# Row statistics of the first token half moved from VectorE to ScalarE in the three generated output projections of a two-layer trunk

## The chip, the cores and the metric

The kernel runs on one NeuronCore of a Trainium2 chip. The metric is the device time of one execution in microseconds (us). The kernel before was timed three times: median 2871.21 us, lowest 2867.52, highest 2874.64. One further execution, the profiled one, took 2872.47 us; every duration below comes from its trace. The engines are called by their short names: PE is TensorE (the matrix engine), DVE is VectorE, ACT is ScalarE, POOL is GpSimd and SP is SyncE, which issues most of the DMAs.

## What is computed

The input `x` has 1024 tokens of width 1024 in float32. It passes two layers. Layer 0 mixes the tokens by a gated delta rule, layer 1 by retention; a convolutional feed-forward block follows in each. Every mixer and every feed-forward block ends in a projection, a scaled residual and a layer norm:

```python
def _standardize(x, eps):
    xf = x.astype(F32)
    mu = jnp.mean(xf, axis=-1, keepdims=True)
    xc = xf - mu
    var = jnp.mean(xc * xc, axis=-1, keepdims=True)
    return xc * lax.rsqrt(var + eps)
...
    for i in range(DEPTH):
        mod = (e @ ada_w[i] + ada_b[i])[:, None, :]
        sh1, sc1, g1, sh2, sc2, g2 = jnp.split(mod, 6, axis=-1)
        y = mixers[i % N_MIXERS](x * (1.0 + sc1) + sh1)
        x = layer_norm(DN_ALPHA * x + (1.0 + g1) * y, ln_g[i, 0], ln_b[i, 0])
        y = conv_ffn(x * (1.0 + sc2) + sh2, ffn_up[i], ffn_conv_w[i], ffn_conv_b[i], ffn_down[i])
        x = layer_norm(DN_ALPHA * x + (1.0 + g2) * y, ln_g[i, 1], ln_b[i, 1])
```

Here `y` is the output of a projection such as `ffn_down` (the last matrix product inside `conv_ffn`) or `ret_w_out` (the last one inside the retention mixer). The change concerns `mu` and `var` of three of the four layer norms: after the feed-forward block of layer 0, after retention, and after the feed-forward block of layer 1, which is the kernel's output.

## The kernel before

**Products.** Every float32 operand is cut into a high part, copied by ACT into a reduced-precision tile (`split`, L89), and a low part, the difference, computed by DVE (L90). Each product of two tiles is then three matmuls (`mma`). A split of a tile of 128 rows and 512 columns is one ACT copy followed by one DVE subtraction, and the matmuls wait for both.

**A projection.** `proj_gen` (L1477 on) computes 1024 tokens by 1024 columns. It uses a form of Strassen's scheme: seven products, called p0 to p6 here, instead of eight. Each product runs over `nj` steps `j` (11 in the feed-forward projections, 8 in the retention projection) of 12 matmuls of 128x512 into four accumulator tiles. `make` prepares the operands of one step: it forms the wanted sum or difference of weight blocks (L1521), splits activations into `ab` and weights into `bb`, and issues the weight load `Br` of three steps further on. The last steps of p6 (`tail`) are held back so that the four row tiles `t` = 0..3 finish one after the other. In the profile the matmuls are L1636.

**The rows' ends.** Tokens come in two halves of 512, each in four row tiles of 128 rows; columns come in two halves `nh` = 0, 1. For each row tile and column half `finish` multiplies by the gate (L1562), adds the scaled residual (L1564) and takes row statistics with BN_STATS (L1565), all on DVE. When both column halves are there, `norm` aggregates them (BN_AGGR, L1570), adds the epsilon (L1571), has POOL raise the result to the power -1/2 (L1572), and normalises the row tile `xt`: on ACT (L321) for the first half of layer 0's projection, on DVE (L323) in the retention projection, and with the output's scale and bias in a mixed way (L1578 to L1586) in the final projection. The first half's column half 0 ends in p2 (p3 in the retention projection), its column half 1 after p4, by a list `later` from which four entries are taken per step of p5. The second half ends with p5 and p6. After that list is empty, `hooks` bring the transposes of the normalised rows (L295), their scaling on ACT (L297) and the splits `hT` for the next stage's matmuls (L110 to L112 in the stage after the retention projection).

**The three calls.** The feed-forward projection of layer 0 lies at about 1160 to 1400 us of the trace, the retention projection at about 2030 to 2230 us, the final one at about 2660 us to the end. They are called the layer-0, the retention and the final projection below. The fourth layer norm uses another function, `proj_ln`, with its own row statistics.

**What sets the order.** The code above is written out by generators; a scheduler of the framework then fixes one static order of instructions for each engine, and each engine runs its own list strictly in that order, waiting by semaphores on the others. So an instruction that is not ready holds up all that stand behind it on its engine. Tiles come from pools of fixed size: `qkv` (20 tiles of 128x512; here `ar`, `Br`, `Bw`, and in the retention projection the sums `c` of L1595), `aux` (`pa`), `cv` (`u2`), and eight banks of PSUM, four of which (`acc`) hold p6 and are then taken over, one by one, by the next stage.

Of the kernel before, what the change touches and what calls it, by code (L numbers as in the profile page):

```python
# [11 lines left out]
AF = mybir.ActivationFunctionType  # L12
ALU = mybir.AluOpType
AX = mybir.AxisListType

P = 128
D = 1024
# [12 lines left out]
LN_EPS = 1e-5  # L30
# [3 lines left out]
def trunk_kernel(ctx: ExitStack, tc, A):  # L34
    nc = tc.nc
    pe, act, dve, pool, sp = nc.tensor, nc.scalar, nc.vector, nc.gpsimd, nc.sync
# [9 lines left out]
    def tl(tag, shape, dt=F32, name=None):  # L46
        return sb.tile(shape, dt, tag=tag, name=name or tag, bufs=BUFS[tag])
# [13 lines left out]
    def mm_tile():  # L61
        return ps.tile([P, HALF], F32, tag="mm", name="mm", bufs=2)

    def sc_tile():
        return ps.tile([P, HALF], F32, tag="sc", name="sc", bufs=2)

    def acc4():
        return [acc_tile(), acc_tile(), acc_tile(), acc_tile()]
# [13 lines left out]
    def hs(half):  # L82
        return slice(half * HALF, (half + 1) * HALF)
# [234 lines left out]
    def normalize(xt, mv, on_act):  # L318
        if on_act:
            dve.scalar_tensor_tensor(mv[:, 2:3], mv[:, 0:1], -1.0, mv[:, 3:4], ALU.mult, ALU.mult)  # L320
            act.activation(xt, xt, AF.Identity, bias=mv[:, 2:3], scale=mv[:, 3:4])  # L321
        else:
            dve.tensor_scalar(xt, xt, mv[:, 0:1], mv[:, 3:4], ALU.subtract, ALU.mult)  # L323
# [483 lines left out]
    def give(tag, n):  # L807
        free[tag] += n
# [468 lines left out]
    c, z = "c", "z"  # L1277
# [199 lines left out]
    def proj_gen(nj, ablk, wsrc, slots, xsrc, G, final, ln_next, tag, ltags, dst, key, mm=pe.matmul, gate=None):  # L1477
# [63 lines left out]
        stats = [[], []]  # L1541
# [15 lines left out]
        def xh(half, t, nh):  # L1557
            x = xts[half][t]
            return x[nh] if isinstance(x, tuple) else x[:, hs(nh)]

        def finish(half, t, nh, c):
            dve.tensor_tensor(c, c, G[nh], ALU.mult)  # L1562
            xv = xh(half, t, nh)
            dve.scalar_tensor_tensor(xv, xv, ALPHA, c, ALU.mult, ALU.add)  # L1564
            dve.bn_stats(stats[half][t][:, nh], xv)  # L1565

        def norm(half, t):
            xt = xts[half][t]
            mv = tl("s8", [P, 4], name="mv")
            dve.bn_aggr(mv[:, 0:2], stats[half][t])  # L1570
            dve.tensor_scalar(mv[:, 2:3], mv[:, 1:2], LN_EPS, None, ALU.add)  # L1571
            pool.tensor_tensor(mv[:, 3:4], mv[:, 2:3], mhalf[:, 0:1], ALU.pow)  # L1572
            if final is None:
                normalize(xt, mv, bal["n"] & 1 << half)
            else:
                (gB, bB), out = final
                r0 = half * HALF + t * P
                dve.scalar_tensor_tensor(mv[:, 2:3], mv[:, 0:1], -1.0, mv[:, 3:4], ALU.mult, ALU.mult)  # L1578
                lo, hi = xh(half, t, 0), xh(half, t, 1)
                act.activation(hi, hi, AF.Identity, bias=mv[:, 2:3], scale=mv[:, 3:4])  # L1580
                dve.scalar_tensor_tensor(lo, lo, mv[:, 0:1], gB[0], ALU.subtract, ALU.mult)
                dve.scalar_tensor_tensor(lo, lo, mv[:, 3:4], bB[0], ALU.mult, ALU.add)
                sp.dma_start(out[r0:r0 + P, hs(0)], lo)
                dve.tensor_mul(hi, hi, gB[1])
                dve.tensor_add(hi, hi, bB[1])
                sp.dma_start(out[r0:r0 + P, hs(1)], hi)  # L1586

        c11, later = [], []
# [22 lines left out]
        def f3(t, acc):  # L1611
            dve.tensor_add(u2[t], acc, u2[t])
            later.append(lambda: finish(0, t, 1, u2[t]))
            later.append(lambda: norm(0, t))

        def f7(t, acc):
            act.activation(u2[t], acc, AF.Copy)
# [39 lines left out]
        for p, (an, bn, fin, side, fresh) in enumerate(prods):  # L1657
            if gate and p < 2 or banks[side] is None:
                banks[side] = acc4() if gate and p < 2 or side == 0 else [sc_tile(), sc_tile(), mm_tile(), mm_tile()]
                if gate and p == 1:  # L1660
                    banks[0] = banks[1]
                    banks[1] = None
            accs = banks[0] if gate and p == 1 else banks[side]
            tail = []
            depth = ltags[3] if p == 6 else 2
            for j in range(nj):
                if gate and p < 2:
                    yield gate(j)
                    yield from take("qkv", 2)
                    give("qkv", 2)  # L1670
                if (p, j) not in ready:
                    make(p, j)
                a, w = ready.pop((p, j))
                if not gate and p == 2 and j % 2 == 0 and j < 8:
                    xload(0, j // 2)
                if not gate and p == 2 and j > 2 and j % 2:
                    finish(0, (j - 3) // 2, 0, p1[(j - 3) // 2])
                if final and p == 3 and j % 2 == 0 and j < 8:
                    xload(1, j // 2)
                if p == 3 and j < 4 and gate:  # L1680
                    xload(0, j)
                    finish(0, j, 0, c11[j])
                if j >= nj - depth:
                    tail.append((j, a, w))
                else:
                    for t in range(4):
                        mma(accs[t], t, a, w, fresh and j == 0, False, mm if p < 2 else pe.matmul if fresh else mm_on)
                        yield 0.0
                for _ in range(-(-20 // (nj - 1)) if p == 6 else 4 if p == 5 else 2):
                    if later:  # L1690
                        later.pop(0)()
                if p == 5 and j > 1 and not later:
                    for _ in range(-(-16 // (nj - 2))):
                        if hooks:
                            hooks.pop(0)()
                bg_step()
            if 0 < p < 6:
                make(p + 1, 0)
            while later:
                later.pop(0)()  # L1700
            if p == 5:
                while hooks:
                    hooks.pop(0)()
            if p == 6:
                pin[0] = None
                preload()
            for t in range(4):
                for j, a, w in tail:
                    mma(accs[t], t, a, w, fresh and j == 0, j == nj - 1, mm if p < 2 else pm_on if p == 6 else pe.matmul if fresh else mm_on)
                fin(t, accs[t])  # L1710
                yield 0.0
            if p == 1:
                yield "P2"
            if p == 4:
                hooks = [] if final else ln_hooks(0, xts[0], tag, ln_next, outs, dst, key, bal["h"])
                if not final:
                    hooks += [lambda t=t: xload(1, t) for t in range(4)]
# [506 lines left out]
```

## Time and profile before

| what | value |
|---|---|
| median of three runs | 2871.21 us |
| profiled execution | 2872.47 us |
| its span, first to last instruction | 2870.7 us |
| mean granted TensorE clock | 0.994 |
| PE busy | 2785.2 us (97%) |
| DVE busy | 2183.3 us (76%) |
| ACT busy | 1294.0 us (45%) |
| POOL busy | 500.2 us (17%) |

Busy time is the time in which an engine executes something. The profiled execution is 1.77 us longer than its span and 1.26 us longer than the median of the three runs. Instructions of one engine overlap a little: an instruction listed with 0.68 us can be followed by the next one 0.60 us after its own start. The distance from start to start is called the pitch here, and it is the pitch that adds up in a row of instructions.

### The profile page before, as it was taken

Reading aid. Unit: us, or ns where it says so; the run is one execution under the profiler, and the core shown is the slowest. Engines: PE = TensorE matmul, PEld = TensorE weight load, DVE = VectorE, ACT = ScalarE, POOL = GpSimd, SP = SyncE. Lnnn points to the kernel's source line nnn. Section 1 sums busy time; section 2 is a strip of 40 time slices with the busy share of each in tenths; the row PEclk is TensorE's granted clock in tenths of the full one; section 3 lists DMA queues with packets and bytes.
Section 4 is the critical chain, followed back from the end, with each engine's and each line's share of the span. In section 5 each row is a group of like instructions: output and inputs, shape, how many; then the busy total and the mean of one; then the engine's idle time right before and its main releaser. Section 6 shows DMA issues by size and latency. Waiting matters only on the chain.

```text
span 2870.7 us, 38939 instructions
## 1 busy us (share of the span) xinstructions
PE 2785.2 (97%) x13594; PEld 2277.0 (79%) x13594; DVE 2183.3 (76%) x3874; ACT 1294.0 (45%) x2377; POOL 500.2 (17%) x517
## 2 busy tenths in 40 slices
PE   8999999999999999999999999999999999999997
PEld 6787878877787788887888887777787778888886
DVE  6887678676788888778677656666788887777869
ACT  3763465344644444546433342222344644444443
POOL 0411321000023233100000002333301033332001
PEclk9999999999999999999999999999999999999999
DMA  8323242174254555945343364665854253444853
GB/s 279 101 90 115 92 140 92 61 250 150 99 180 168 192 183 172 336 126 180 128 147 119 121 204 153 200 196 160 275 194 147 74 194 132 143 139 161 320 150 118
DMA packets 254292, 465.31 MB, mean 162 GB/s; under 512 B 24400, under 2 KB 81104, under 8 KB 254096
## 3 DMA queue, kind: packets, MB, share of 16 engines
q1 hardware_dynamic: 219776, 407.50, 43.0%
q10 hardware_dynamic: 31488, 46.15, 4.4%
q0 software_dynamic: 2832, 9.18, 0.8%
q8 instruction: 107, 1.75, 0.2%
q14 instruction: 89, 0.73, 0.1%
HBM read 346.86 MB, written 115.87 MB: 161 GB/s over the span
## 4 chain that ended last, share of the span: by engine, by line
PE 56%; DVE 21%; DMA 11%; ACT 6%; issue 5%; POOL 1%; SPq 0%; ACTq 0%; DVEq 0%; POOLq 0%
PE acc L747 10%; PE acc L1340 5%; PE acc L110 4%; PE sc L747 4%; PE acc L111 4%; PE acc L112 4%; PE sc L1340 3%; PE acc L1636 3%; DMA mvw<-in_ada_w 3%; DVE o L1787 3%; DMA wr<-in_ffn_up 2%; PE mm L747 2%; DVE wb L90 2%; DVE qkv L507 2%; DVE mm L1394 1%
## 5 line engine op out<-in xcount | busy, mean ns | idle before, releaser
L747 PE MATMUL acc<-hT,wh 128*128 128x512 f32 x960 | 299.7, 393 | 0.0
L1636 PE MATMUL acc<-bb,ab 128*128 128x512 f32 x984 | 229.8, 392 | 6.5 <-DVE ab L90 4.1
L89 ACT ACTIVATE ab<-ar 128x512 fp32r<-128x512 f32 x210 | 131.1, 629 | 217.0 <-PE mm L316 55.1
L1636 PEld LDWEIGHTS acc<-bb,ab 128*128 128x128 f32 x984 | 183.0, 188 | 48.6 <-DVE ab L90 4.7
L747 PEld LDWEIGHTS acc<-hT,wh 128*128 128x128 f32 x960 | 182.5, 190 | 35.6
L1340 PE MATMUL acc<-T,wb 128*128 128x512 f32 x840 | 202.0, 389 | 0.4 <-DVE wb L90 0.4
L90 DVE TENSOR_TENSOR ab<-ar,ab 128x512 fp32r<-128x512 f32 x210 | 148.7, 715 | 68.5 <-ACT ab L89 68.1
L747 PE MATMUL acc<-hT,wl 128*128 128x512 f32 x480 | 197.3, 411 | 1.2 <-ACT sq L531 0.7
L89 ACT ACTIVATE wb<-mm 128x512 fp32r<-128x512 f32 x216 | 124.4, 597 | 163.0 <-DVE mm L1394 150.1
L1340 PEld LDWEIGHTS acc<-T,wb 128*128 128x128 f32 x840 | 157.5, 188 | 33.8 <-ACT o L1788 1.1
L90 DVE TENSOR_TENSOR wl<-wr,wh 128x1024 fp32r<-128x1024 f32 x95 | 118.6, 1249 | 74.3 <-ACT wh L89 72.6
L1818 POOL TENSOR_TENSOR o<-o 128x512 f32<-128x512 f32 x80 | 119.0, 1496 | 270.1 <-DVE o L1810 167.9
L90 DVE TENSOR_TENSOR wb<-wr,wb 128x512 fp32r<-128x512 f32 x162 | 114.2, 706 | 65.7 <-ACT wb L89 65.6
L89 ACT ACTIVATE wh<-wr 128x1024 fp32r<-128x1024 f32 x95 | 100.6, 1060 | 138.3 <-PE acc L747 61.4
L1787 DVE SCALAR_TENSOR_TENSOR o<-g,vc,o 128x512 f32<-128x512 f32 (+2 forms) x176 | 152.2, 875 | 8.9 <-ACT o L1782 7.7
L90 DVE TENSOR_TENSOR wb<-mm,wb 128x512 fp32r<-128x512 f32 x216 | 144.5, 682 | 7.4 <-ACT wb L89 7.4
L89 ACT ACTIVATE wb<-wr 128x512 fp32r<-128x512 f32 x162 | 101.2, 626 | 95.5 <-PE acc L1340 28.8
L1394 DVE TENSOR_TENSOR mm<-wr 128x512 f32<-128x512 f32 x108 | 83.9, 777 | 71.4 <-DMA wr<-in_ffn_up 58.2
L747 PE MATMUL acc<-wh,hT 128*128 128x512 f32 x384 | 134.3, 412 | 2.1 <-DVE vv L90 2.1
L1410 ACT ACTIVATE pc<-acc 128x512 f32<-128x512 f32 x143 | 84.4, 591 | 111.8 <-PE acc L1340 63.6
L252 DVE SCALAR_TENSOR_TENSOR ada<-mvw,e,ada 128x512 f32<-128x512 f32 x140 | 105.8, 755 | 24.0 <-DMA mvw<-in_ada_w 23.8
L110 PE MATMUL acc<-T,wb 128*128 128x512 f32 x292 | 114.9, 394 | 3.6 <-DVE wb L90 3.3
(677 smaller groups left out, 7356.2 us busy)
## 6 DMA issues: line engine op xcount, KB each, us to landing
wr<-in_ffn_up SPq DMA_DIRECT2D x92, 512.0 KB, 3.9
mvw<-in_ada_w SPq DMA_DIRECT2D x80, 512.0 KB, 4.3
ad<-o SPq DMA_DIRECT2D x154, 256.0 KB, 2.3
ar<-ad SPq DMA_DIRECT2D x154, 256.0 KB, 4.2
Br<-in_ffn_down SPq DMA_DIRECT2D x88, 256.0 KB, 5.2
wr<-in_ret_wv SPq DMA_DIRECT2D x32, 512.0 KB, 3.6
ar<-od SPq DMA_DIRECT2D x56, 256.0 KB, 4.5
wr<-in_gdn_wqkv SPq DMA_DIRECT2D x24, 512.0 KB, 3.9
```

Of the source, the lines that this page charges most:

```text
L89: anchor["sp"] = act.activation(dst_h, src, AF.Copy)
L90: eng.tensor_tensor(dst_l, src, dst_h, ALU.subtract)
L110: mm(acc, wl[:, k], hl[0], start=first, stop=False)
L111: mm(acc, wh[:, k], hl[1], start=False, stop=False)
L112: mm(acc, wh[:, k], hl[0], start=False, stop=last)
L252: dve.scalar_tensor_tensor(a, wr[:, kk], e[:, k:k + 1], a, ALU.mult, ALU.add)
L747: pq(pe.matmul(out, lhsT, rhs, start=start, stop=stop), cost or COST[out.shape[-1]])
L1340: return pe.matmul(*a, skip_group_check=True, **kw)
L1394: dve.tensor_tensor(t, x, y, op)
L1636: return pe.matmul(*args, skip_group_check=True, **kw)
L1787: dve.scalar_tensor_tensor(tv, gv[:, c0 - j:c1 - j], w[:, 2 - j:3 - j], tv, ALU.mult, ALU.add)
L1818: (dve if fp == 0 else pool).tensor_tensor(o[d], o[x], o[y], op)
```

## The change

For the first token half alone, BN_STATS is replaced by an ACT copy that also sums its row (`accum_out`); what it copies goes nowhere, into a tile that is no longer needed (`spare`). A new step `mean` forms minus the mean, scaled by 1/32, with two tiny DVE operations, and then has ACT sum the squares of (row minus mean)/32 for each column half, which gives the variance. `norm` then needs one tiny DVE operation in place of BN_AGGR and the old L1571. On the list `later`, the mean of row tile t-1 and the normalisation of row tile t-2 stand behind the end of row tile t. In the final projection two entries per step of p5 are taken from the list, instead of four. The second half is as before.

```diff
-            dve.bn_stats(stats[half][t][:, nh], xv)
+            if half:
+                dve.bn_stats(stats[half][t][:, nh], xv)
+            else:
+                act.activation(c, xv, AF.Copy, accum_out=stats[0][t][:, 0, nh:nh + 1])
+                spare[t, nh] = c
+
+        spare = {}
+
+        mvs = {}
+
+        def mean(t):
+            mv = mvs[t] = tl("s8", [P, 4], name="mv")
+            st = stats[0][t]
+            dve.tensor_scalar(mv[:, 1:2], st[:, 0, 0:1], st[:, 0, 1:2], -D ** -1.5, ALU.add, ALU.mult)
+            dve.tensor_scalar(mv[:, 0:1], mv[:, 1:2], -D ** 0.5, None, ALU.mult)
+            for nh in range(2):
+                act.activation(spare[t, nh], xh(0, t, nh), AF.Square, bias=mv[:, 1:2], scale=D ** -0.5,
+                               accum_out=st[:, 1, nh:nh + 1])
 
         def norm(half, t):
             xt = xts[half][t]
-            mv = tl("s8", [P, 4], name="mv")
-            dve.bn_aggr(mv[:, 0:2], stats[half][t])
-            dve.tensor_scalar(mv[:, 2:3], mv[:, 1:2], LN_EPS, None, ALU.add)
+            mv = tl("s8", [P, 4], name="mv") if half else mvs[t]
+            if half:
+                dve.bn_aggr(mv[:, 0:2], stats[half][t])
+                dve.tensor_scalar(mv[:, 2:3], mv[:, 1:2], LN_EPS, None, ALU.add)
+            else:
+                st = stats[0][t]
+                dve.tensor_scalar(mv[:, 2:3], st[:, 1, 0:1], st[:, 1, 1:2], LN_EPS, ALU.add, ALU.add)
...
         def f3(t, acc):
             dve.tensor_add(u2[t], acc, u2[t])
             later.append(lambda: finish(0, t, 1, u2[t]))
-            later.append(lambda: norm(0, t))
+            if t:
+                later.append(lambda: mean(t - 1))
+            if t > 1:
+                later.append(lambda: norm(0, t - 2))
+            if t == 3:
+                later.extend([lambda: mean(3), lambda: norm(0, 2), lambda: norm(0, 3)])
...
-                for _ in range(-(-20 // (nj - 1)) if p == 6 else 4 if p == 5 else 2):
+                for _ in range(-(-20 // (nj - 1)) if p == 6 else (2 if final else 4) if p == 5 else 2):
```

The scheduler's order changes inside the three projections only. Lines behind the change have new numbers: the new ACT copy is L1568 and the squares are L1581; the tiny operations of `mean` are L1578 and L1579 and that of `norm` is L1592; BN_STATS of the second half is L1566.

The first place is DVE at the retention projection's end, where the second half's row tiles leave PSUM. `acc` are the four accumulators of p6, `xt` rows of the second half, `wl` and `hT` splits for the next stage. Before:

```order
L1625 TENSOR_TENSOR acc_18311<-acc_18311,pa_17751 128x512
L1565 BN_STATS st_19357<-xt_19355 128x6
L1565 BN_STATS st_19360<-xt_19358 128x6
L90 TENSOR_TENSOR wl_19683<-wr_19680,wh_19682 128x1024
L1562 TENSOR_TENSOR acc_18311<-acc_18311,rowb_17095 128x512
L1625 TENSOR_TENSOR acc_18312<-acc_18312,pa_17751 128x512
L90 TENSOR_TENSOR hT_19208<-t2_19206,hT_19208 128x512
L90 TENSOR_TENSOR wl_19717<-wr_19714,wh_19716 128x1024
L1564 SCALAR_TENSOR_TENSOR xt_19355<-xt_19355,acc_18311 128x512
L1625 TENSOR_TENSOR acc_18313<-acc_18313,pa_17752 128x512
L1562 TENSOR_TENSOR acc_18312<-acc_18312,rowb_17095 128x512
L90 TENSOR_TENSOR hT_19218<-t2_19216,hT_19218 128x512
```

At the same place now (the first accumulator is called `acc_18323`):

```order
L1562 TENSOR_TENSOR acc_18323<-acc_18323,rowb_17107 128x512
L90 TENSOR_TENSOR hT_19338<-t2_19336,hT_19338 128x512
L1651 TENSOR_TENSOR acc_18325<-acc_18325,pa_17764 128x512
L90 TENSOR_TENSOR wl_19741<-wr_19738,wh_19740 128x1024
L1566 BN_STATS st_19387<-xt_19385 128x6
L1651 TENSOR_TENSOR acc_18326<-acc_18326,pa_17764 128x512
L1562 TENSOR_TENSOR acc_18324<-acc_18324,rowb_17107 128x512
L1566 BN_STATS st_19401<-xt_19399 128x6
L90 TENSOR_TENSOR wl_19772<-wr_19769,wh_19771 128x1024
L1564 SCALAR_TENSOR_TENSOR xt_19379<-xt_19379,acc_18323 128x512
L1562 TENSOR_TENSOR acc_18325<-acc_18325,rowb_17107 128x512
L1562 TENSOR_TENSOR acc_18326<-acc_18326,rowb_17107 128x512
```

The reading of the first accumulator (L1564 with `acc_18311`, now `acc_18323`), which is the last use of that bank, has moved behind more statistics, more splits and the other accumulators' first steps.

The second place is DVE at the very end of the kernel, from the last L1562 on; `xt_24076` and so on are output rows. Before:

```order
L1562 TENSOR_TENSOR acc_23291<-acc_23291,rowb_20840 128x512
L1570 BN_AGGR mv_25161<-st_24178 128x2
L1584 TENSOR_TENSOR xt_24076<-xt_24076,rowb_23273 128x512
L1584 TENSOR_TENSOR xt_24125<-xt_24125,rowb_23273 128x512
L1564 SCALAR_TENSOR_TENSOR xt_24225<-xt_24225,acc_23291 128x512
L1571 TENSOR_SCALAR mv_25161<-mv_25161 128x1
L1581 SCALAR_TENSOR_TENSOR xt_24174<-xt_24174,mv_25161,rowb_23273 128x512
L1585 TENSOR_TENSOR xt_24076<-xt_24076,rowb_23276 128x512
L1585 TENSOR_TENSOR xt_24125<-xt_24125,rowb_23276 128x512
L1565 BN_STATS st_24229<-xt_24225 128x6
```

Now:

```order
L1562 TENSOR_TENSOR acc_23315<-acc_23315,rowb_20864 128x512
L1588 BN_AGGR mv_25197<-st_24202 128x2
L1606 TENSOR_TENSOR xt_24149<-xt_24149,rowb_23300 128x512
L1564 SCALAR_TENSOR_TENSOR xt_24249<-xt_24249,acc_23315 128x512
L1589 TENSOR_SCALAR mv_25197<-mv_25197 128x1
L1602 SCALAR_TENSOR_TENSOR xt_24198<-xt_24198,mv_25197,rowb_23297 128x512
L1566 BN_STATS st_24253<-xt_24249 128x6
```

Three output steps of 128x512 (two of L1584 and one of L1585, now L1605 and L1606) have moved ahead of the last L1562.

The third place is ACT in p5 of the layer-0 projection, where it normalises the first half (L321) among the splits. Before:

```order
L89 ACTIVATE ab_12112<-ar_12109 128x512
L89 ACTIVATE bb_12115<-Br_11984 128x512
L321 ACTIVATE xt_11138<-xt_11138,mv_11919 128x1024
L89 ACTIVATE ab_12155<-ar_12152 128x512
L89 ACTIVATE bb_12158<-Br_12032 128x512
L89 ACTIVATE bb_12374<-Br_12268 128x512
```

Now:

```order
L89 ACTIVATE ab_12081<-ar_12078 128x512
L89 ACTIVATE bb_12084<-Br_11939 128x512
L1568 ACTIVATE u2_11669,st_11293<-xt_11291 128x512
L1581 ACTIVATE pa_10622,st_11189<-xt_11187,mv_11953 128x512
L1581 ACTIVATE u2_11653,st_11189<-xt_11187,mv_11953 128x512
L321 ACTIVATE xt_11138<-xt_11138,mv_11922 128x1024
L1581 ACTIVATE pa_10623,st_11241<-xt_11239,mv_11965 128x512
L1581 ACTIVATE u2_11661,st_11241<-xt_11239,mv_11965 128x512
L89 ACTIVATE ab_12124<-ar_12121 128x512
L89 ACTIVATE bb_12127<-Br_11979 128x512
```

Sums and squares now stand ahead of splits in ACT's list.

## The prediction

> **What bounds the kernel now.** I read the page's totals and its chain first, then the engines' busy time by stretches at the three projections that the change touches, then there PE's waits, and last the rows of DVE, PE and ACT around each wait.
>
> ```profile
> span 2870.7 us, 38939 instructions
> PE 2785.2 (97%) x13594; PEld 2277.0 (79%) x13594; DVE 2183.3 (76%) x3874; ACT 1294.0 (45%) x2377; POOL 500.2 (17%) x517
> PE 56%; DVE 21%; DMA 11%; ACT 6%; issue 5%; POOL 1%; SPq 0%; ACTq 0%; DVEq 0%; POOLq 0%
> ```
>
> PE is busy for 97% of the span: 85.5 us are all that could go if no matmul changes. Of the chain that ended last DVE has 21%, so DVE is the partner to look at, in the stages where it is full. The next rows are the stretches around the projections' ends: time, then the busy time of PE, PEld, DVE, ACT and POOL. The first three lie in the layer-0 projection, the fourth in the retention projection, the last in the final one.
>
> ```profile
> 1300.00:1320.00 20.00, 18.86 (x83) 15.31 (x82) 15.21 (x27) 5.88 (x10) 0.64 (x1) 1.00 0.43 143
> 1320.00:1340.00 20.00, 19.98 (x92) 16.23 (x92) 16.99 (x38) 16.44 (x26) 3.54 (x4) 1.00 0.83 287
> 1340.00:1360.00 20.00, 17.00 (x84) 13.09 (x83) 20.00 (x35) 17.62 (x32) 0.59 (x1) 1.00 0.33 105
> 2150.00:2210.00 60.00, 56.75 (x258) 44.78 (x257) 60.00 (x105) 31.48 (x50) 5.66 (x6) 1.00 0.43 143
> 2800.00:2860.00 60.00, 55.82 (x244) 45.27 (x242) 60.00 (x116) 22.99 (x39) 9.58 (x6) 0.99 0.34 111
> ```
>
> DVE has no gap at all in the last three, while PE loses 3 to 4 us in each. ACT is half idle in the retention and final projections, but not in the layer-0 one (16.44 and 17.62 of 20). PE's waits, for the windows 1306 to 1370, 2148 to 2226 and 2830 us to the end:
>
> ```profile
> PE acc L1636 <- DVE ab L90: 3.0, 3, 2.1
> PE acc L1636 <- DVE bb L90: 1.1, 1, 1.1
> ```
>
> ```profile
> PE acc L1636 <- ACT bb L89: 1.2, 1, 1.2
> PE mm L452 <- ACT bt L454: 1.0, 2, 0.5
> PE mm L295 <- DVE xt L323: 0.9, 1, 0.9
> PE acc L110 <- DVE xt L1564: 0.7, 1, 0.7
> PE acc L1636 <- DVE ab L90: 0.3, 1, 0.3
> ```
>
> ```profile
> PE acc L1636 <- DVE ab L90: 0.8, 2, 0.6
> ```
>
> So PE loses 4.1 us to DVE in the layer-0 projection, and 3.1 us in the retention projection before the next stage's own L452. In the final one the tail after the last matmul belongs to DVE.
>
> **What the change costs and saves, in general.** The rows that give the prices:
>
> ```profile
> L1565 DVE BATCH_NORM_STATS2 st<-xt x48: 665/683/695, 1227.8 to 2862.1; 128x6 f32<-128x512 f32 x48
> 2171.82 0.20 DVE L1570 BATCH_NORM_AGGREGATE mv<-st 128x2 f32<-128x12 f32 x1
> 2171.94 0.10 DVE L1571 TENSOR_SCALAR mv<-mv 128x1 f32<-128x1 f32 x1
> 2172.55 0.14 DVE L1571 TENSOR_SCALAR mv<-mv 128x1 f32<-128x1 f32 x1
> 2172.61 0.68 DVE L90 TENSOR_TENSOR bb<-Br,bb 128x512 fp32r<-128x512 f32 x1
> 1357.38 1.28 DVE L90 TENSOR_TENSOR ab<-ar,ab 128x512 fp32r<-128x512 f32 x2
> ```
>
> Two DVE operations of 128x512 take 1.28 us where one takes 0.68, so the pitch is 0.60; BN_STATS, at 0.683, is of the same kind. BN_AGGR has a pitch of 0.12 (2171.94 less 2171.82), a tiny operation about 0.06. Each projection loses 8 BN_STATS and 4 BN_AGGR and gains 8 tiny operations (4 L1571 become 4 L1592): 8 x 0.60 + 4 x 0.12 - 8 x 0.06 = 4.80 us of DVE. Half of the BN_STATS, those of column half 0, stand early (p2 or p3), where DVE has gaps and PE does not wait for it: worth nothing. What counts in p5 is 4 x 0.60 + 0.48 - 0.48 = 2.4 us. ACT gains 8 sums and 8 squares, each followed by a read of the accumulator:
>
> ```profile
> 1351.09 1.15 ACT L89 ACTIVATE ab<-ar 128x512 fp32r<-128x512 f32 x2
> L1580 ACT ACTIVATE xt<-xt,mv x8: 802/814/817, 2821.5 to 2865.2; 128x512 f32<-128x512 f32 x8
> L531 ACT ACTIVATE sq<-acc x64: 257/285/321, 108.7 to 534.6; 128x128 f32<-128x128 f32 x64
> L531 ACT ACTIVATION_READ_ACCUMULATOR sq<-acc x64: 193/218/254, 108.8 to 534.8; 128x1 f32 x64
> ```
>
> A plain copy of 128x512 has a pitch near 0.53 (1.15 less about 0.62). A square with one pointer operand lies between that and L1580's 0.81 with two; the read adds between nothing and 0.22. My estimate is 0.62 for a sum and 0.71 for a square; the ends are 0.53 and 1.03. In p5 that is 4 x 0.62 + 8 x 0.71 = 8.2 us of ACT (6.4 to 12.4). The Trainium skill, page "ScalarE: Activation LUTs", section "Rules for kernel authors", says to do additions and multiplications on VectorE and not on ScalarE, which speaks against the change. This trace has the same price on both at this shape (copy 0.63 on ACT, 0.68 on DVE), so that here the question is only which engine is late.
>
> **Layer-0 projection.** The rows of PE's largest wait and of DVE ahead of it:
>
> ```profile
> 1358.12 2.12 PE L1636 MATMUL acc<-bb,ab 128*128 128x512 f32 x8 [2.08 <-DVE ab L90]
> 1335.70 0.69 DVE L1521 TENSOR_TENSOR Br<-Br,Bw 128x512 f32<-128x512 f32 x1 [1.98 <-DMA Br<-in_ffn_down]
> ```
>
> From 1335.70 to 1357.38, 21.7 us, DVE runs without a gap to the `ab` split for which PE waits 2.08 us. In the new list three rows of 0.60 fewer stand between the two: 1.8 us. What DVE saves before 1335.70 is lost to the DMA wait there, except that this load is itself issued behind DVE splits; of the 2.4 us saved I count 1.0. Together -2.8 us. The ends: -0.5, if only one BN_STATS ahead of the first wait (1.1 us) counts, and -4.1, all that PE waits there. ACT's added 8.2 us stand against 3.6 idle us in 1320 to 1340 and 14.1 in the 20 us ahead; the `ab` copy (1351.09) is 6.3 us ahead of DVE's use of it (1357.38), which covers what lag is left.
>
> **Retention projection.** Here the moved order decides.
>
> ```profile
> 2196.67 0.67 DVE L1564 SCALAR_TENSOR_TENSOR xt<-xt,acc 128x512 f32<-128x512 f32 x1
> 2198.47 0.47 PE L110 MATMUL acc<-hT,wl 128*128 128x512 f32 x1
> 2203.32 0.50 PE L110 MATMUL acc<-hT,wl 128*128 128x512 f32 x1 [0.74 <-DVE xt L1564]
> 2222.29 1.04 PE L452 MATMUL mm<-cst,xt 128*128 128x128 f32 x8
> 2225.49 0.69 DVE L90 TENSOR_TENSOR 12_19794<-bt,12_19794 128x512 fp32r<-128x512 f32 x1 [9.61 <-ACT 12_19794 L89]
> L90 DVE TENSOR_TENSOR wl<-wr,wh 128x1024 fp32r<-128x1024 f32 x95 | 118.6, 1249 | 74.3 <-ACT wh L89 72.6
> 2843.41 13.22 PE L1636 MATMUL acc<-bb,ab 128*128 128x512 f32 x57 [0.23 <-DVE ab L90]
> ```
>
> The next stage's first matmul (2198.47) takes over the bank whose last reader is L1564 of row tile 0 (2196.67 to 2197.34); its second unit did wait for the next bank. DVE is full from p4's end on, so that L1564 comes when the rows ahead of it are done. The new list has there, from L1612 (L1633 now) on, 11 more rows of 128x512, one more `wl` split of 128x1024 (1.25, pitch near 1.14), 8 more tiny ones and 4 BN_AGGR fewer: 6.6 + 1.1 + 0.5 - 0.5 = 7.8 us. Those are the transposes' `hT` splits, two L1521, and the statistics and rests of the second half. L1564 then starts at 2196.67 + 7.8 = 2204.5 and the bank is free at 2205.1. All of p6 and of the transposes now stands before the first L110 on PE, and nothing behind it can overtake it. The stage's first 96 matmuls need 96 x 0.23 = 22.0 us (57 matmuls of this size took 13.22 in the last of these rows, from the final projection): they end at 2227.1 instead of 2222.29, so +4.8 us. DVE's saved 2.4 us come behind that place and fall into its own idle time (9.61 us before 2225.49). The ends: -2.4, if DVE gets to this place early after all and PE's 3.1 us of waits mostly go, and +7.8, if the delay of the bank comes through whole.
>
> **Final projection.**
>
> ```profile
> 2857.69 0.69 DVE L1562 TENSOR_TENSOR acc<-acc,rowb 128x512 f32<-128x512 f32 x1
> 2867.02 0.69 DVE L1585 TENSOR_TENSOR xt<-xt,rowb 128x512 f32<-128x512 f32 x1
> ```
>
> The last matmul ends at 2856.63 (2843.41 + 13.22, the row above), DVE reaches the last accumulator at 2857.69 and needs 10.0 us more to 2867.71; the rest to 2870.7 is the last output's DMA. DVE is full from before 2800 on, so its 2.4 us come off its end if the accumulator is ready: three output rows (3 x 0.60) now precede that L1562, which would start at 2857.69 - 2.4 + 1.8 = 2857.1, still behind the last matmul. I take -2.3 (ends: 0, if ACT's squares hold up a split by 2 us, and -3.2, if PE's two waits of 0.8 us there go and help too).
>
> **The sum.** -2.8 + 4.8 - 2.3 = -0.3 us against the profiled execution's 2872.47 (1.77 of it lie outside the span and stay): 2872.17. The median was 1.26 below that execution: 2870.9 us.
>
> **Rivals.** (A) *The bank does not bite*: if DVE reaches L1564 early enough, PE's waits go in all three places, 4.1 + 3.1 + 3.2 = 10.4 us: 2860.8 us. For it: DVE is full exactly where PE waits. Against it: the new order of DVE puts 7.8 us more in front. (B) *Slower, by ACT's list in p5*: a square waits for DVE's `mean`, and all splits queued behind it on ACT wait with it; DVE's low parts and PE's matmuls wait for those. In the layer-0 projection ACT has only 5.9 idle us of 40 from 1320 on. It decides from the point where ACT's lag exceeds the 6.3 us of lead. At the upper end of my price (12.4 us), less the 3.6 idle, the lag is 8.8, 2.5 over the lead, and each hold-up by `mean` adds to it; if the layer-0 projection turns from -2.8 to +4, the retention projection takes its upper end of 7.8 for the same reason and the final one gains nothing, the sum is +11.8 and the time 2883.0 us. (C) *The change does nothing*: what DVE gives back is idle time everywhere and the bank's delay is taken up by slack behind it: 2871.2 us. Against it: DVE's end in the final projection is the kernel's end.
>
> **How the numbers follow.** A measurement of this kernel can tell some 0.3%, 8.6 us, from no change. Forecast as summed 0.60; A 0.12; B 0.13; C 0.15. The sum's own range: the ends of the three terms move it between about -8 and +7 when they don't all fall together, and the three runs lay 3.7 us below to 3.4 above their median. I give 2863 to 2880, which leaves out most of A and of B. A counts as faster, less what falls short of 8.6 us (0.11), B as slower, less the same (0.12); the rest, 0.77, is within 0.3%.
>
> **What would show it right or wrong.** In the new profile: no L1565 left but 24 BN_STATS under L1566, 48 ACT instructions more; PE's wait ahead of the layer-0 projection's late `ab` split shrunk from 2.08 to below 1 us; a wait of 5 to 8 us of PE's first L110 for L1564 near 2197 to 2205, which is new; the last DVE row 8 to 10 us behind the last matmul and 2 us earlier against the start of the stage. The forecast is wrong if that bank wait is absent, or if PE waits for ACT's or DVE's splits in p5 by more than 2 us where it did not before.

## The result and the profile after

The changed kernel has a median of 2878.99 us over seven runs (2876.86 to 2886.16), the kernel before 2869.08 us over seven (2862.00 to 2874.64): a ratio of 1.0036, 95% interval 1.0022 to 1.0049, so about 10 us slower, and by the interval 6 to 14. Forecast were 2870.9 us and a range of 2863 to 2880: the median lies just inside that range, but the sum forecast no change. The profiled execution of the changed kernel took 2886.16 us, 7 us above its own median; stages are compared below, not totals.

The page's head and chain of the changed kernel:

```profile
span 2884.4 us, 39042 instructions
PE 2789.0 (97%) x13594; PEld 2279.1 (79%) x13594; DVE 2177.4 (75%) x3862; ACT 1324.6 (46%) x2473; POOL 504.0 (17%) x517
PE 57%; DVE 19%; DMA 12%; ACT 6%; issue 4%; POOL 1%; SPq 0%; ACTq 0%; DVEq 0%; POOLq 0%
```

The operations changed as the diff says: ACT executes 96 instructions more (48 sums and squares, each with a read of the accumulator) and is 30.6 us busier. DVE is 5.9 us less busy and has 19% of the chain where it had 21%.

Where the time went can be read without any guess from PE alone: both kernels execute 13594 matmuls, so the start of the n-th one can be subtracted from the start of the n-th one before. That difference is 2.7 us ahead of the layer-0 projection (the programs are the same up to there: scatter), 3.5 us behind it, 4.1 us ahead of the end of the retention projection, 17.1 us behind it and 14.9 us at the final projection. The retention projection's end alone costs 13.0 us. The 2.2 us regained behind it are not an effect of the change: the other kernels below regain 0.8 to 3.4 us there against the same profile, those with the old operations too. PE's waits at the retention projection's end (engine, tile, line, what it waited for: us, times, longest), changed kernel, 2150 to 2245 us:

```profile
PE mm L295 <- ACT t L297: 5.3, 1, 5.3
PE acc L110 <- DVE xt L1564: 4.9, 1, 4.9
PE mm L295 <- DVE xt L323: 1.5, 1, 1.5
PE mm L452 <- ACT bt L454: 1.0, 2, 0.5
PE acc L1662 <- DVE ab L90: 0.8, 2, 0.6
```

The wait for L1564, the bank's last reader, is the one that was forecast: 0.7 us before, 4.9 now. The first line is new and was not forecast: transposes (L295) that wait 5.3 us for ACT's scaling (L297). The rows around it, of GpSimd, ACT, PE and DVE, each with its idle time and releaser in brackets:

```profile
2183.45 8.82 POOL L90 TENSOR_TENSOR hT<-t,hT 128x512 fp32r<-128x512 f32 x1 [8.03 <-ACT hT L89]
```

```profile
2192.31 0.78 ACT L297 ACTIVATE t<-mm,fh,fs 128x512 f32<-128x512 f32 x1 [7.22 <-POOL hT L90]
```

```profile
2193.14 1.11 PE L295 MATMUL mm<-cst,xt 128*128 128x128 f32 x4 [5.33 <-ACT t L297]
2214.81 0.79 PE L110 MATMUL acc<-hT,wl 128*128 128x512 f32 x1 [4.88 <-DVE xt L1564]
2215.40 0.63 PE L111 MATMUL acc<-hT,wh 128*128 128x512 f32 x1
2215.82 0.63 PE L112 MATMUL acc<-hT,wh 128*128 128x512 f32 x1
2239.31 1.03 PE L452 MATMUL mm<-cst,xt 128*128 128x128 f32 x8
```

```profile
2152.69 1.28 DVE L1633 TENSOR_TENSOR u<-sc,u 128x512 f32<-128x512 f32 x2
2189.86 1.29 DVE L1562 TENSOR_TENSOR pa<-pa,rowb 128x512 f32<-128x512 f32 x2
2193.63 0.69 DVE L90 TENSOR_TENSOR hT<-t,hT 128x512 fp32r<-128x512 f32 x1 [2.48 <-ACT hT L89]
2201.78 0.70 DVE L1651 TENSOR_TENSOR acc<-acc,pa 128x512 f32<-128x512 f32 x1 [1.50 <-PE acc L1662]
2214.06 0.69 DVE L1564 SCALAR_TENSOR_TENSOR xt<-xt,acc 128x512 f32<-128x512 f32 x1
```

One of the eight `hT` splits of this stage is done by GpSimd (a setting of the kernel that the change doesn't touch). It took 1.30 us before:

```profile
2191.44 1.30 POOL L90 TENSOR_TENSOR hT<-t,hT 128x512 fp32r<-128x512 f32 x1 [14.60 <-ACT hT L89]
```

In the changed kernel the transposes stand earlier in PE's list, between the matmuls of p6, and so the split comes earlier too, into a stretch in which DVE runs splits and additions without a gap. It then takes 8.82 us and ends at 2192.27, 1.1 us after DVE has run dry (2189.86 + 1.29 = 2191.15). Until then it holds one of the three `t` tiles, ACT can't scale the next transposed tile, and PE stands in front of a transpose with p6's matmuls queued behind it. At last DVE itself has nothing left but a split that waits for ACT, and that gap lets GpSimd end. The Trainium skill, page "SBUF — State Buffer", section "Who interferes with whom", says that a VectorE instruction with two SBUF inputs contends with a GpSimd instruction that reads SBUF, and one with at most one SBUF input, outside the modes that use two ports, does not; the experiments below show the same on this kernel.

What that does to the bank stands in DVE's list. Before, the stretch from p4's end to the bank's last reader began here:

```profile
2148.18 1.28 DVE L1612 TENSOR_TENSOR u<-sc,u 128x512 f32<-128x512 f32 x2
```

From this row to the L1564 at 2196.67 DVE took 48.5 us, without a pause. In the changed kernel it takes 61.4 us (2152.69 to 2214.06), 12.9 more, where the forecast had 7.8 for the added rows. DVE now stands still for 2.48 us around the end of GpSimd's split, for 1.50 us until p6, held up on PE by its wait of 5.3 us, gives an accumulator, and for five shorter waits: 4.6 us in all.

The third part is PE's clock. The stretches around the two waits (time, PE, PEld, DVE, ACT, POOL, then the granted clock):

```profile
2184.00:2194.00 10.00, 4.67 (x27) 3.88 (x25) 7.52 (x13) 2.78 (x5) 8.27 (x1) 0.95 0.15 52
2194.00:2204.00 10.00, 10.00 (x45) 8.24 (x44) 8.20 (x12) 6.57 (x11) 0.00 (x0) 0.87 0.36 121
2204.00:2214.00 10.00, 5.93 (x27) 4.57 (x25) 9.98 (x15) 3.42 (x4) 0.00 (x0) 0.98 0.52 197
2214.00:2224.00 10.00, 9.19 (x29) 7.37 (x30) 9.48 (x23) 0.00 (x0) 3.21 (x4) 0.68 0.28 107
```

Behind each long wait the granted clock is down (0.87 and 0.68; before, it was 1.00 in this stage): in the trace it is 0.50 from 2193.1 to 2196.5 and from 2213.6 to 2220.4. The first matmuls of the next stage follow each other by 0.42 us (2215.82 less 2215.40) instead of 0.23. PE waits 12.5 us in this stage where it waited 3.1 before, 9.4 more (both without L452); the lower clock takes half of the time from 2193.14 to 2196.5 and from 2214.81 to 2220.4, 4.5 us more. Their sum, 13.9, is near the 13.0 measured. The Trainium skill, page "TensorE: Matmul & The Clock Gate", section "Why this matters for your kernels", gives half clock after a gap of more than about 3 us between matmuls. These two waits agree, and so do the other seven of over 3 us that PE has in this stage in the kernels below. But it is not the whole rule: in five of those kernels half clock also followed waits of only 1.3 to 1.9 us, and in others such waits were followed by none.

The other two projections. PE's waits in the layer-0 projection, 1306 to 1376 us, changed kernel:

```profile
PE acc L1662 <- DVE ab L90: 2.4, 2, 1.5
PE mm L295 <- ACT t L297: 2.0, 1, 2.0
PE acc L1662 <- DVE bb L90: 0.7, 1, 0.7
```

That is 5.1 us, where it was 4.1. The wait of 2.08 us for the late `ab` split is gone, as forecast; the one for a transposed tile took its place. Here is the scaling on ACT that this tile needs, and then the two ends of the final projection:

```profile
1360.29 1.45 ACT L297 ACTIVATE t<-mm,fh,fs 128x512 f32<-128x512 f32 x2 [1.82 <-DVE hT L90]
```

```profile
2858.12 13.23 PE L1662 MATMUL acc<-bb,ab 128*128 128x512 f32 x57 [1.01 <-DVE ab L90]
2880.75 0.69 DVE L1606 TENSOR_TENSOR xt<-xt,rowb 128x512 f32<-128x512 f32 x1
```

The scaling waits 1.82 us for an `hT` split of DVE. At the end of the kernel DVE's last row ends 10.1 us behind the last matmul (2881.44 less 2871.35), where it was 11.1.

### The profile page after: what moved, and what is told of

Same layout as the page of the kernel before. It is cut to its first block, busy times and chain, and to the rows that moved or that the text cites. A ratio compares the mean times of both kernels' runs of the same rounds, so it can differ in the third digit from the quotient of the medians.

```text
span 2884.4 us, 39042 instructions
## 1 busy us (share of the span) xinstructions
PE 2789.0 (97%) x13594; PEld 2279.1 (79%) x13594; DVE 2177.4 (75%) x3862; ACT 1324.6 (46%) x2473; POOL 504.0 (17%) x517
## 4 chain that ended last, share of the span: by engine, by line
PE 57%; DVE 19%; DMA 12%; ACT 6%; issue 4%; POOL 1%; SPq 0%; ACTq 0%; DVEq 0%; POOLq 0%
PE acc L747 9%; PE acc L1340 5%; PE acc L110 4%; PE acc L111 4%; PE acc L112 4%; PE acc L1662 4%; PE sc L747 3%; PE sc L1340 3%; DMA mvw<-in_ada_w 2%; DVE o L1813 2%; PE mm L747 2%; DVE wb L90 2%; DMA wr<-in_ffn_up 2%; DVE qkv L507 2%; DVE mm L1394 1%
## 5 line engine op out<-in xcount | busy, mean ns | idle before, releaser
L1394 DVE TENSOR_TENSOR mm<-wr 128x512 f32<-128x512 f32 x108 | 87.6, 811 | 68.8 <-DMA wr<-in_ffn_up 56.2
L252 DVE SCALAR_TENSOR_TENSOR ada<-mvw,e,ada 128x512 f32<-128x512 f32 x140 | 106.3, 759 | 24.5 <-DMA mvw<-in_ada_w 24.3
L110 PE MATMUL acc<-T,wb 128*128 128x512 f32 x292 | 114.4, 392 | 5.2 <-DVE wb L90 5.2
```

The source lines that it names most:

```text
L110: mm(acc, wl[:, k], hl[0], start=first, stop=False)
L252: dve.scalar_tensor_tensor(a, wr[:, kk], e[:, k:k + 1], a, ALU.mult, ALU.add)
L1394: dve.tensor_tensor(t, x, y, op)
```

## The experiments

Each kernel is the changed one (or the one before, where it says so) with the edit shown; `new` is a flag by which a projection keeps its old statistics and list. All were timed against the kernel before on the same chip. The difference of the retention projection's end by the n-th matmul, +13.0 us for the changed kernel, is called the stage difference. It is read from one profile of each kernel; the three kernels below that keep the old statistics in that projection and hold no tiles there have 0.0, +0.2 and +0.3. The times are less sharp: where one is called some us below the changed kernel (by the ratios and by the medians), the interval of its ratio overlaps that of the changed kernel (1.0022 to 1.0049), and the stage difference is what tells the two apart.

**One projection at a time.** The edit of the first kernel; the second has `new = not gate`.

```diff
+        new = bool(gate)
-            if half:
+            if half or not new:
                 dve.bn_stats(stats[half][t][:, nh], xv)
...
+            if not new:
+                later.append(lambda: norm(0, t))
+                return
```

> The change in the retention projection alone; the layer-0 and the final projection take their statistics as before. Theory A (the loss comes from the retention projection, where the new order puts all transposes into p6 and the next stage's first bank behind most of DVE's list; the other two gain little): 8 to 13 us slower than before, so as slow as the whole change or slower. Rival B (ACT's list of sums and squares in p5 delays splits in all three projections alike): a third to a half of the loss, 3 to 5 us slower.

Measured: 2882.22 us, ratio 1.0044 (1.0032 to 1.0056), about 12.6 us slower; stage difference +12.6. GpSimd's split took 7.87 us there.

> The change in the layer-0 and the final projection, the retention projection as before. Theory A: between 2 us faster and 1 us slower than before (about 1 us gained in the final tail, about nothing in the layer-0 projection). Rival B: 4 to 7 us slower than before.

Measured: 2869.51 us, ratio 0.9995 (0.9986 to 1.0004); stage difference of the retention projection +0.3. So the loss is the retention projection's, nearly all of it, and the two others together gain nothing that can be measured. Rival B, as far as it means all three projections, falls.

**GpSimd's split.** The setting `rh` gives the number of `hT` splits that GpSimd does in this stage.

```diff
-"rn": 0, "rh": 1,
+"rn": 0, "rh": 0,
```

> The whole change, and the one split of a transposed tile that GpSimd does in the retention projection (8.8 us in the profile of the changed kernel, 1.3 before) goes to VectorE. Theory A in the form that this long split holds PE up: PE's 5.3 us wait for a transposed tile goes, the first bank comes earlier by some 3 to 5 us, and the time is 4 to 8 us below the changed kernel. Rival C (the split is only a name on a wait that has another cause, VectorE's full list): within 2 us of the changed kernel.

Measured: 2874.13 us, ratio 1.0024 (1.0015 to 1.0033), 3 to 5 us below the changed kernel; stage difference +6.5. PE's wait for the transposed tile is gone, the wait for the bank is not:

```profile
2177.40 0.44 PE L295 MATMUL mm<-cst,xt 128*128 128x128 f32 x2 [1.49 <-DVE xt L323]
2208.45 0.79 PE L110 MATMUL acc<-hT,wl 128*128 128x512 f32 x1 [5.11 <-DVE xt L1564]
```

DVE now goes from p4's end to the bank's last reader in 55.0 us, without a pause of more than 0.2 us. The order is not quite that of the changed kernel: three `wl` splits stand ahead of that reader, not four (some 1.1 us), as in the kernel with the gap below.

> The kernel before with that same split on VectorE. Both theories: within 1.5 us of the kernel before, since the split took 1.3 us there and nobody waited for it long; 0.6 us more on a full VectorE.

Measured: 2868.19 us, ratio 0.9999 (0.9990 to 1.0008), stage difference 0.0. In the old order the split cost nothing that can be measured, although it holds DVE up in its turn. A `wl` split beside it took 2.02 us in the kernel before, where such a split takes 1.25 in the mean; without GpSimd's split no row there is stretched.

```profile
2191.80 2.02 DVE L90 TENSOR_TENSOR wl<-wr,wh 128x1024 fp32r<-128x1024 f32 x1
```

**More room for the tile that GpSimd holds.**

```diff
-            "wr": 2, "wh": 2, "wl": 2, "t2": 3,
+            "wr": 2, "wh": 2, "wl": 2, "t2": 4,
```

> The whole change with four buffers instead of three for the scaled transposed tiles (t2). Theory A (GpSimd's split can't finish while VectorE runs two-input operations without a gap; the tile that it holds stops ScalarE's next scaling, and with it PE's transposes): GpSimd's split stays long, 5 us or more, but PE's 5.3 us wait shrinks to under 2, and the time is 3 to 6 us below the changed kernel (near 2874). Rival C (the wait has another cause): no difference beyond 2 us.

Measured: 2880.14 us, ratio 1.0038 (1.0025 to 1.0052), stage difference +14.6. My expectation was wrong. GpSimd and PE:

```profile
2171.00 11.89 POOL L90 TENSOR_TENSOR hT<-t,hT 128x512 fp32r<-128x512 f32 x1 [7.98 <-ACT hT L89]
```

```profile
2183.75 1.11 PE L295 MATMUL mm<-cst,xt 128*128 128x128 f32 x4 [6.95 <-ACT t L297]
2204.90 0.79 PE L110 MATMUL acc<-hT,wl 128*128 128x512 f32 x1 [5.16 <-DVE xt L1564]
```

One more buffer gave ACT, and so DVE, one more tile to work on before they stopped; DVE's gap came later, and GpSimd's split ended only with it, after 11.89 us. The split's length follows DVE's next gap, not its own work; a buffer only puts the stop off.

**A gap for GpSimd.** Two BN_STATS whose result nobody uses, behind GpSimd's split, on the same tile: more work for DVE, but with one input.

```diff
         split(ht[0], ht[1], tmp, eng)
+        if eng is pool:
+            for _ in range(2):
+                dve.bn_stats(tl("st", [P, 2, 6], name="idle")[:, 0], tmp)
         return ht
```

> The whole change, and behind GpSimd's split VectorE gets two BN_STATS on the same scaled tile whose result nobody uses: 1.2 us more on a full VectorE, but operations with one input. Theory A (one-input operations let GpSimd in): GpSimd's split takes 1.3 to 3 us instead of 8.8, PE's 5.3 us wait goes, and the time is 3 to 6 us below the changed kernel, in spite of the added work. Rival C: 0 to 2 us slower than the changed kernel.

Measured: 2874.69 us, ratio 1.0019 (1.0010 to 1.0028), 4 to 5 us below the changed kernel; stage difference +6.1. GpSimd and DVE:

```profile
2179.99 2.47 POOL L90 TENSOR_TENSOR hT<-t,hT 128x512 fp32r<-128x512 f32 x1 [8.99 <-ACT hT L89]
```

```profile
2180.63 0.68 DVE L1649 TENSOR_TENSOR pa<-pa 128x512 f32<-128x512 f32 x1
2181.23 1.28 DVE L302 BATCH_NORM_STATS2 idle<-t 128x6 f32<-128x512 f32 x2
2182.43 1.27 DVE L1649 TENSOR_TENSOR pa<-pa 128x512 f32<-128x512 f32 x2
```

The split ends at 2182.46, with the two BN_STATS (2181.23 to 2182.51), in a row of DVE without a gap. So 1.2 us of added DVE work halved the loss of the stage. It also explains the 1.30 us of the kernel before, whose split ran beside BN_STATS of the second half.

**What moved the order.** In the retention projection the change holds the four tiles `c` of the pool `qkv` from p3 to p5, as the place for what the squares write. Three kernels tell this from the operations. First, both squares of a row tile write into the later of its two spare tiles, so that `c` is free in p3:

```diff
-                act.activation(spare[t, nh], xh(0, t, nh), AF.Square,
+                act.activation(spare[t, 1], xh(0, t, nh), AF.Square,
```

> The whole change, but both squares of a row tile write into the later of its two spare tiles, so that the retention projection gives its four tiles c back in p3. Same operations, but another order: from p4's end to the first bank's last reader there are 70 rows of 128x512 on VectorE instead of 79 and 3 big splits instead of 4 (before: 68 and 3). Theory A, order decides: the first bank comes 6 to 7 us earlier than in the changed kernel, and the time is 5 to 10 us below it (2869 to 2874). Rival B (sums and squares in ScalarE's list): within 2 us of the changed kernel, as ScalarE does the same work.

Measured: 2870.19 us, ratio 1.0004 (0.9995 to 1.0013); stage difference +0.9. PE's waits there, 2150 to 2222 us:

```profile
PE acc L1662 <- ACT u L1643: 1.7, 1, 1.7
PE mm L295 <- ACT t L297: 0.8, 1, 0.8
PE acc L1662 <- DVE ab L90: 0.4, 1, 0.4
PE mm L295 <- DVE xt L323: 0.4, 1, 0.4
```

No wait for the bank at all, and 3.3 us in all, with the same sums and squares on ACT. The 1.7 us in which p6 waits for ACT to empty its bank (L1643) are in neither the kernel before nor the changed one; that ACT's longer list causes them is likely, but not shown. If it does, rival B's mechanism exists at that size. GpSimd's split is long here too, and costs nothing that can be seen, since PE waits only 0.8 us for a scaled tile:

```profile
2186.91 4.97 POOL L90 TENSOR_TENSOR hT<-t,hT 128x512 fp32r<-128x512 f32 x1 [7.64 <-ACT hT L89]
```

Second, the list's later normalisation alone, with BN_STATS on DVE in the retention projection:

```diff
-            if half:
+            if half or gate:
                 dve.bn_stats(stats[half][t][:, nh], xv)
...
         def mean(t):
+            if gate:
+                return
```

> The whole change, but the retention projection's first half takes its statistics by BN_STATS on VectorE as before; only the later normalisation of the list remains there. VectorE's and PE's order at the end of that projection is then that of the kernel before. Theory A: as fast as the change without the retention projection, 2867 to 2871. A rival by which the later normalisation itself costs: 3 us or more above that.

Measured: 2871.66 us, ratio 1.0010 (1.0001 to 1.0019), a little above what was expected, and 4 us above the kernel without the change in this projection if the ratios are compared (0.9995 there), as the rival would have it. But the stage difference is +0.2, so whatever it is, it doesn't come from there. GpSimd's split took 1.29 us.

Third, the kernel before, with nothing but four one-column reads that hold the tiles `c`:

```diff
             pool.tensor_tensor(mv[:, 3:4], mv[:, 2:3], mhalf[:, 0:1], ALU.pow)
+            if gate and not half:
+                act.activation(tl("st", [P, 2, 6], name="idle")[:, 0, 0:1], c11[t][:, 0:1], AF.Identity, bias=mv[:, 2:3])
```

> The kernel before with nothing moved to ScalarE: only four one-column ScalarE reads of the four tiles c of the retention projection, put at the first half's normalisation, so that these tiles are held from p3 to p5 as in the change. The order moves by that alone: 76 rows of 128x512 on VectorE from p4's end to the first bank's last reader (before 68, changed 79), and the next stage's 96 matmuls stand in one piece behind it. Theory D (the held tiles move the order, and the order costs the time): 3 to 8 us slower than before, with a wait of PE's first L110 for L1564 of 2 us or more. Rival (the moved operations cost it): within 1.5 us of before.

Measured: 2869.49 us, ratio 1.0010 (0.9999 to 1.0021), which is unclear; stage difference +2.1. GpSimd's split and PE's waits, 2140 to 2222 us:

```profile
2181.66 6.40 POOL L90 TENSOR_TENSOR hT<-t,hT 128x512 fp32r<-128x512 f32 x1 [10.67 <-ACT hT L89]
```

```profile
PE mm L295 <- DVE xt L323: 2.2, 2, 1.3
PE acc L110 <- DVE xt L1564: 1.2, 1, 1.2
```

Holding the tiles moves the order in the direction of the change, without any of its operations, and brings its signs in small: a split of 6.40 us, a longer wait for the bank (1.2 us instead of 0.7), transposes that wait longer. It gives 2 us of the 13, not the 3 to 8 that I expected. The held tiles are necessary for the loss (the kernel without them has +0.9), but not enough. All 32 transposes stand ahead of the first L110 in both of these kernels too (24 before), so that alone is not the loss; only the held tiles and the new operations together put 79 rows of 128x512 and a fourth `wl` split ahead of the bank's last reader. DVE has no gap beside this split. It ends 1.24 us after the start of L1627 (2186.82), one of whose two inputs is an accumulator in PSUM.

**Late transposes.** The change with the held tiles, the transposes written out later:

```diff
-                if p == 5 and j > 1 and not later:
-                    for _ in range(-(-16 // (nj - 2))):
+                if p == 5 and j > (5 if gate else 1) and not later:
+                    for _ in range((12 if gate and j == 6 else 8 if gate else -(-16 // (nj - 2)))):
```

> The whole change with held tiles, but the transposes of the retention projection are written out only from step 6 of p5 on. VectorE's list ahead of the first bank's last reader is shorter than in the change (75 rows of 128x512 and 3 big splits instead of 79 and 4). Theory A (rows ahead of the bank, and transposes ahead of p6's matmuls): 2 to 8 us below the changed kernel. Rival: no difference.

Measured: 2872.83 us, ratio 1.0022 (1.0009 to 1.0035), 4 to 6 us below the changed kernel; stage difference +7.2. PE's waits, 2150 to 2232 us:

```profile
PE mm L295 <- ACT t L297: 4.2, 2, 3.8
PE mm L295 <- DVE xt L323: 1.9, 1, 1.9
PE acc L110 <- DVE xt L1564: 1.6, 1, 1.6
PE acc L1662 <- ACT u L1643: 0.4, 1, 0.4
```

The wait for the bank shrinks from 4.9 to 1.6 us with the rows ahead of it, by order alone. PE's waits for transposes stay (6.1 us), and GpSimd's split takes 5.84 us.

**The best form.** No held tiles and GpSimd's split on DVE:

```diff
-"rn": 0, "rh": 1,
+"rn": 0, "rh": 0,
...
-                act.activation(spare[t, nh], xh(0, t, nh), AF.Square,
+                act.activation(spare[t, 1], xh(0, t, nh), AF.Square,
```

> The whole change without the held tiles and with GpSimd's split on VectorE: the candidate for the best form of the change. Theory D: as the kernel before or up to 2 us faster, 2866 to 2870. Rival B (ScalarE's list): 2872 or more.

Measured: 2866.79 us, ratio 1.0001 (0.9990 to 1.0012); stage difference -1.0. This is the change without its accident, and it gains nothing that can be measured.

## Why the prediction was wrong, point by point

- **Retention projection, forecast +4.8, measured +13.0 us.** The place and the first link were right: the next stage waits for the bank, because its last reader moved back in DVE's list (4.9 us, forecast 5 to 8). The price of the added rows was about right too: DVE's way to the bank grew by 8.3 us without its pauses, and the forecast's terms add up to 7.7 (it says 7.8). The step that failed is "DVE is full from p4's end on, so that L1564 comes when the rows ahead of it are done". With it went that p6 and its transposes run through. Transposes inside p6 can stop p6, and did, for 5.3 us, since they depend on ACT, ACT on a tile that GpSimd holds, and GpSimd on a gap of DVE; DVE then stood still for 4.6 us itself. So L1564 started at 2214.06, not at 2204.5: 5.5 us later, if one takes off the 4.1 us by which this profile was late already. The second thing left out is the clock: from the first L110 to the first L452 24.5 us passed (2214.81 to 2239.31), not 22.0, so 2.5 more. 4.8 + 5.5 + 2.5 = 12.8. The upper end that I gave, +7.8, took the delay of the bank as the worst case, and no chain across engines.
- **What GpSimd's split runs beside.** The prediction did not ask beside which DVE operations the one split on POOL would now run. It is the same instruction with 1.30, 2.47, 4.97, 5.84, 6.40, 7.87, 8.82 and 11.89 us, according to when DVE next has a gap or an operation with at most one SBUF input.
- **Layer-0 projection, forecast -2.8, measured nothing.** The stage difference was +0.7, and in the other kernels with the new statistics there -0.2 to +2.4, in the three further ones with the old statistics -0.5 to +4.0: the scatter is larger than the term. The wait that I forecast to shrink, 2.08 us for the late `ab` split, did: all four profiles with the old statistics have it, and of the nine with the new ones only one has a wait like it (1.90, with four buffers `t2`). The step that failed is to count it as gained. In six of the nine PE waits 1.85 to 1.99 us for a scaled transposed tile a few matmuls earlier instead, behind the same full DVE, and in two more than 3 us for a split of a weight block.
- **Final projection, forecast -2.3, measured -1.0 in this profile.** From one and the same late matmul to DVE's end, the nine profiles with the new form give 33.5 us on average (32.8 to 34.3), the four with the old one 34.0. So the gain is about 0.5 us. Weight loads are not the reason, as DVE waits 8.5 us for them in this projection and waited 8.4 before. What the forecast did not have is a new wait of DVE for GpSimd's power (L1593) at the very end. Five of the nine profiles have it twice (0.32 and 0.44 us) and gain 0.1 us on average, two have it once and gain 0.8, and the two without it, the changed kernel's own among them, gain 1.1 and 1.2. Why these two do not reach 2.3 stays open.
- **Rivals.** B had the right sign and about the right price (2883.0 us) with another mechanism, which is luck: in the one place where a wait for ACT's list may show alone it is 1.7 us. A (DVE reaches the bank early) is wrong, since the bank wait is there. C (nothing gained) holds for two of the three projections.

What stays open: why holding the tiles and moving the statistics add up to more than their parts in the scheduler's order; I saw it in the orders and the times, and did not follow it into the scheduler. DVE's busy time fell by 5.9 us where the operations taken away and added account for some 13. Part of the difference is work that the change does not touch and that took longer in this profile (L1394 is busy for 87.6 us, before 83.9); the rest I did not follow.

## What to carry to other kernels

Where an order is made by a scheduler from tile lifetimes, a tile used as a dump for unwanted output is not free: holding four of twenty from p3 to p5 moved the critical reader of a bank, and with the moved operations cost 13 us of a stage that loses 0.9 without it. Before trusting a row of moved instructions, follow every instruction that moved with them to all engines it needs, and ask beside what it will now run; an offloaded split on GpSimd is short only beside gaps of VectorE or operations with one SBUF input, and a long one costs time only where another engine waits for its tile. And when a wait goes, ask what the waiting engine will need next: in the layer-0 projection it was the next tile of the same full engine.

## What the runs showed of the hardware

A GpSimd subtraction of 128x512 that takes 1.3 us beside one-input operations took 5.0 to 11.9 us in six kernels, beside an unbroken row of VectorE operations with two SBUF inputs. In four of them it ended 1.12 us after VectorE ran dry (2191.15 and 2192.27 in the changed kernel). In the two others, and in the kernel with the two added BN_STATS, where it took 2.5 us, it ended 1.23 or 1.24 us after the start of an operation with at most one SBUF input, with no gap in the row: a BN_STATS or an addition to an accumulator in PSUM. It holds VectorE up in its turn: a split of 128x1024 beside it took 2.02 us, with a mean of 1.25.

PE's matmuls of 128x512 came every 0.42 us instead of 0.23 behind a wait of 4.9 us, and the mean granted clock in the 10 us behind it was 0.68. A sum of 128x512 with its accumulator read took 0.61 to 0.65 us of ScalarE from start to start, and a square 0.71: the estimates of 0.62 and 0.71 were right.
